# Moving memsets behind the first copies of an attention kernel, and making its first transposes plain matmuls

## The chip, the cores and the metric

One core of a Trainium2 chip. The metric is the device time of one execution in microseconds, median of several executions. The trace of a profiled execution gives the *span*, first to last instruction; it is mostly about 2 us less than the device time of the same run.

## The reference

```python
batch, n_heads, seq_len, head_dim = 4, 8, 1024, 64     # q, k, v; bias is (1, 1, 1024, 1024); all float32
scores = (1 / sqrt(64)) * q @ k.T + bias
attn   = exp(scores - max) / (sum(exp(scores - max)) + 1e-8)
return attn @ v
```

## The kernel before

Heads are worked on in pairs. Scores are computed transposed, in pieces of 512 columns of PSUM, called banks below, three at a time; ScalarE takes the exponential of three banks in one instruction (128x1536, 1.45 us as drawn). The bias enters as a factor, `exp(bias)`, which VectorE multiplies in. v carries a 65th column of ones, so that the last matmul also sums the exponentials. TensorE transposes q and k, and `mask` blanks the other head's half of q.

Everything after the head of the program is emitted by a small model of the engines, written in Python, that picks at each step the instruction that could start first. Its constants `T0` (when the head ends) and `COLD` (until when TensorE costs double) shape that order. This is the head (cut):

```python
nc.sync.dma_start(out=k0f[:, :, :2]...)    # k and q of the first pair, f32, by hardware queues
nc.scalar.dma_start(out=q0f[0]...); nc.sync.dma_start(out=q0f[1]...); nc.sync.dma_start(out=k0f[:, :, 2:]...)
nc.vector.memset(warm[:], 0.0); nc.vector.memset(zeros[:], 0.0)
make_identity(nc, ident[:])
nc.gpsimd.dma_start(kr0 second half); nc.gpsimd.dma_start(qr0 second half); nc.gpsimd.dma_start(btraw first half)
for t in range(2):
    nc.vector.memset(qT0[t * D:(t + 1) * D, 1 - t, :HQ], 0.0)
    for u in range(2):
        nc.vector.memset(mask[t * D:(t + 1) * D, u, :], 1.0 if t == u else 0.0)
nc.gpsimd.memset(vall[:, :, :, D:D1], 1.0)             # the ones, 256 scattered elements per partition
load_v(0); load_qk(1); nc.gpsimd.dma_start(btraw second half); load_v(1); load_qk(2)
wm = ps_s.tile([P, 3, HQ], F32, tag="s", name="wm")
for i in range(6):                                     # warm-up matmuls
    nc.tensor.matmul(wm[:, i % 3, :], zeros[:, :P], zeros[:], start=True, stop=True)
k_first(0, nc.scalar.copy, nc.scalar.copy, "xb")       # cast, transpose, copy of k, chunks 0 and 1
c_a = q_first(0, "xa"); c_b = q_first(1, "xb")         # cast and transpose q of both heads
c_a(); c_b()                                           # copy them out of PSUM
s_fill(0); s_exp(0)                                    # scores and exponential of one bank
k_first(2, nc.vector.tensor_copy, nc.vector.tensor_copy, "xa")
s_fill(1); s_exp(1)                                    # two banks
...                                                    # from here on by the model, three banks each
# the piece of k, chunks 4 to 7, that the fourth exponential needs, is copied in transpose_pe():
nc.vector.tensor_copy(dst[:, half * QC:(half + 1) * QC, :], px[:])          # "the k copy" below
```

The softmax here doesn't subtract the row's maximum and nothing guards it: scores larger than these inputs give would overflow.

## Time and profile before

| | before |
|---|---|
| device time, median of 3 (later 6) runs | 252.03 us (252.06) |
| span of the profiled run | 249.9 us |
| ScalarE busy | 239.0 us, 96% |
| starts of the first four score exponentials | 6.77, 8.43, 9.71, 11.07 us |
| clock of TensorE rises to full | 9.85 us |

From the page of the kernel before: busy time of each engine, and the chain that ended last, by engine.

```profile
PE 228.8 (92%) x3097; PEld 141.1 (56%) x3152; DVE 221.2 (89%) x380; ACT 239.0 (96%) x180; POOL 54.0 (22%) x73
...
ACT 87%; PE 6%; DVE 4%; issue 2%; DVEq 0%; ACTq 0%
```

ScalarE is the engine that the end waits for. From the third exponential (9.71 us) on it runs practically without a break, so the total follows the time at which that unbroken run can begin. What comes before is the head. Its timeline, lines picked; columns: start and duration in us, engine, line, operation, output and inputs, count, and in brackets the idle time before with what ended it.

```profile
3.46 1.70 DVE L258 CAST qr<-q0f 128x256 bf16<-128x256 f32 x2
...
3.54 1.26 POOL L237 MEMSET vall<- 128x256 bf16 x1
...
5.01 0.83 PE L261 MATMUL px<-ident,qr 128*64 128x128 bf16 x8 [0.59 <-DVE qr L258]
...
5.68 0.88 DVE L262 COPY qT<-px 64x512 bf16<-64x512 bf16 x2 [0.53 <-PE px L261]
...
7.36 2.31 PE L129 MATMUL ps<-qT,kT 128*128 128x512 bf16 x5
...
9.61 0.51 PE L89 MATMUL px<-ident,kr 128*64 128x128 bf16 x8
9.71 2.81 ACT L136 ACTIVATE E<-ps 128x1536 bf16<-128x1536 f32 x2 [0.26 <-PE ps L129]
...
10.16 0.42 DVE L102 COPY kT<-px 128x512 bf16<-128x512 bf16 x1 [2.40 <-PE px L89]
```

The two casts of q are of one shape, but the first takes 1.50 us and the second 0.275 (they overlap a little in the 1.70 drawn); the first lies over GpSimd's memset. The five score matmuls from 7.36 us start 0.43 us apart, twice the 0.215 us of those from 11.21 us on: I read that as TensorE at half clock. (Where the trace has a record of a low clock, after its last fall at 248.78 us, the share is 0.5.) The last line is the k copy that the fourth exponential needs: VectorE had been idle for 2.40 us and waited for TensorE's transposes.

### The profile page before, as it was taken

Reading aid. Unit: us, or ns where it says so; the run is one execution under the profiler, and the core shown is the slowest. Engines: PE = TensorE matmul, PEld = TensorE weight load, DVE = VectorE, ACT = ScalarE, POOL = GpSimd, SP = SyncE. Lnnn points to the kernel's source line nnn. Section 1 sums busy time; section 2 is a strip of 40 time slices with the busy share of each in tenths; the row PEclk is TensorE's granted clock in tenths of the full one; section 3 lists DMA queues with packets and bytes.
Section 4 is the critical chain, followed back from the end, with each engine's and each line's share of the span. In section 5 each row is a group of like instructions: output and inputs, shape, how many; then the busy total and the mean of one; then the engine's idle time right before and its main releaser. Section 6 shows DMA issues by size and latency. Waiting matters only on the chain.

```text
span 249.9 us, 7123 instructions
## 1 busy us (share of the span) xinstructions
PE 228.8 (92%) x3097; PEld 141.1 (56%) x3152; DVE 221.2 (89%) x380; ACT 239.0 (96%) x180; POOL 54.0 (22%) x73
## 2 busy tenths in 40 slices
PE   6969999999999999999999999999998999999893
PEld 2346655556566665565565555566665555665552
DVE  7229799899999998999999999999999999998884
ACT  3799999999999999999999999999999999999991
POOL 8753213054004132203150130416000000000000
PEclk9999999999999999999999999999999999999999
DMA  7999979369905987923958194949911102020112
GB/s 153 179 221 183 192 85 149 32 112 154 149 4 104 113 104 114 122 84 52 164 77 93 45 117 95 117 98 108 107 42 43 45 0 88 3 84 3 62 45 64
DMA packets 48175, 23.79 MB, mean 95 GB/s; under 512 B 34448, under 2 KB 44048, under 8 KB 47888
## 3 DMA queue, kind: packets, MB, share of 16 engines
q0 software_dynamic: 42272, 14.42, 52.8%
q1 hardware_dynamic: 5584, 8.72, 9.8%
q8 instruction: 24, 0.39, 0.6%
q10 hardware_dynamic: 288, 0.20, 0.3%
q14 instruction: 7, 0.06, 0.1%
HBM read 29.36 MB, written 8.39 MB: 151 GB/s over the span
## 4 chain that ended last, share of the span: by engine, by line
ACT 87%; PE 6%; DVE 4%; issue 2%; DVEq 0%; ACTq 0%
ACT E L136 84%; PE ps L129 4%; ACT eb L149 3%; PE po L186 1%; DVE mask L236 1%; DVE qr L258 1%; DVE E L155 1%; PE px L89 0%; DVE qT L262 0%; DVE qT L98 0%; PE px L261 0%; DVE E L158 0%; DVE qT L234 0%; DVE oall L206 0%; PE px L254 0%
## 5 line engine op out<-in xcount | busy, mean ns | idle before, releaser
L136 ACT ACTIVATE E<-ps 128x1536 bf16<-128x1536 f32 (+2 forms) x172 | 230.1, 1681 | 3.3 <-PE ps L129 3.3
L129 PE MATMUL ps<-qT,kT 128*128 128x512 bf16 x457 | 135.3, 381 | 11.3 <-ACT E L136 4.6
L186 PEld LDWEIGHTS <-E 128*128 128x128 bf16 x2048 | 82.9, 98 | 39.1 <-DVE E L158 2.7
L158 DVE TENSOR_TENSOR E<-E,eb 128x2048 bf16<-128x2048 bf16 x80 | 96.5, 1217 | 1.0 <-ACT E L136 0.5
L186 PE MATMUL po<-vall,E 128*128 128x65 bf16 x2048 | 92.5, 194 | 2.4 <-DVE E L161 0.8
L129 PEld LDWEIGHTS <-kT 128*128 128x128 bf16 x512 | 45.3, 97 | 43.0 <-issue 8.1
L161 DVE TENSOR_TENSOR E<-E,eb 128x1024 bf16<-128x1024 bf16 x88 | 58.2, 683 | 0.9 <-ACT E L136 0.6
L75 POOL DMA_DIRECT2D kr<-in_k_dram x15 | 10.5, 701 | 94.6 <-PE px L89 92.2
L81 POOL DMA_DIRECT2D vall<-in_v_dram x32 | 28.2, 884 | 6.1 <-DMA btraw<-in_bias_dram 4.0
L206 DVE TENSOR_TENSOR oall<-po,rs 128x256 f32<-128x256 f32 x63 | 26.7, 425 | 2.2
L98 DVE TENSOR_TENSOR qT<-px,mask 128x1024 bf16<-128x1024 bf16 x31 | 21.3, 688 | 4.6 <-PE px L89 4.0
L102 DVE COPY kT<-px 128x512 bf16<-128x512 bf16 x31 | 13.1, 422 | 10.2 <-PE px L89 10.0
L76 POOL DMA_DIRECT2D qr<-in_q_dram x15 | 10.8, 719 | 19.4 <-PE px L89 18.5
L196 DVE RECIPROCAL rs<-po 128x4 f32<-128x4 f32 x64 | 11.3, 177 | 3.4 <-PE po L186 3.1
L89 PEld LDWEIGHTS <-qr 128*64 128x64 bf16 x248 | 7.8, 109 | 9.4 <-issue 8.0
L89 PE MATMUL px<-ident,qr 128*64 128x128 bf16 x248 | 12.8, 225 | 0.1
L89 PE MATMUL px<-ident,kr 128*64 128x128 bf16 x248 | 12.9, 226 | 0.0
L89 PEld LDWEIGHTS <-kr 128*64 128x64 bf16 x248 | 8.0, 110 | 6.1 <-issue 4.2
L149 ACT ACTIVATE eb<-pb 128x2048 bf16<-128x2048 bf16 x4 | 7.5, 1882 | 0.0
L144 PE MATMUL pb<-ident,btraw 128*128 128x128 bf16 x64 | 4.6, 225 | 1.2 <-ACT eb L149 0.6
L144 PEld LDWEIGHTS <-btraw 128*128 128x128 bf16 x64 | 4.5, 146 | 1.6 <-issue 1.3
L155 DVE TENSOR_TENSOR E<-E,eb 128x1024 bf16<-128x1024 bf16 (+1 forms) x6 | 4.6, 775 | 0.6 <-ACT E L136 0.6
(35 smaller groups left out, 22.3 us busy)
## 6 DMA issues: line engine op xcount, KB each, us to landing
out_dram<-oall SPq DMA_DIRECT2D x30, 256.0 KB, 2.0
vall<-in_v_dram POOLq DMA_DIRECT2D x32, 128.0 KB, 5.6
kr<-in_k_dram POOLq DMA_DIRECT2D x15, 256.0 KB, 3.9
qr<-in_q_dram POOLq DMA_DIRECT2D x15, 256.0 KB, 5.3
btraw<-in_bias_dram POOLq DMA_DIRECT2D x2, 1024.0 KB, 10.7
out_dram<-oall SPq DMA_DIRECT2D x3, 128.0 KB, 1.7
k0f<-in_k_dram SPq DMA_DIRECT2D x2, 128.0 KB, 3.3
q0f<-in_q_dram ACTq DMA_DIRECT2D x1, 128.0 KB, 2.5
```

The source lines that it names most:

```text
L81: nc.gpsimd.dma_start(out=vall[:, 2 * pr + t, :, :D], in_=vf[pr, :, t])
L89: nc.tensor.transpose(px[t * D:(t + 1) * D, c, :], src[:, t, half * QC + c, :], ident[:])
L98: nc.vector.tensor_tensor(dst[:, :, half * HQ:(half + 1) * HQ], px.rearrange("p c q -> p (c q)").unsqueeze(1).to_broadcast([P, 2, HQ]), ma ...
L102: nc.vector.tensor_copy(dst[:, half * QC:(half + 1) * QC, :], px[:])
L129: nc.tensor.matmul(ps[:, j, :], kT[:, kc, :], qT[:, h, qh * HQ:(qh + 1) * HQ], start=True, stop=b not in late_bias)
L136: nc.scalar.activation(e_at(slots[g][0], n), open_ps.pop(("S", g))[:, :n, :], ACTF.Exp, scale=scale)
L149: nc.scalar.activation(eb[:, qh, k0:k0 + 4, :], open_ps.pop(("B", qh, k0))[:, :4, :], ACTF.Exp)
L158: nc.vector.tensor_tensor(e, e, eb[:, qh, kc:kc + 2, :].unsqueeze(2).to_broadcast([P, 2, 2, HQ]), op=ALU.mult)
L161: nc.vector.tensor_tensor(e, e, eb[:, qh, kc:kc + 1, :].to_broadcast([P, n, HQ]), op=ALU.mult)
L186: nc.tensor.matmul(acc[:, i, :], e[:, 0, i * P:(i + 1) * P], vall[:, 2 * pr + h, kc, :], start=(kc == 0 and i == 0), stop=(kc == NCH - 1), ...
L196: nc.vector.reciprocal(rs[:], acc[:, :, D:D1])
L206: nc.vector.tensor_tensor(oall[:, c0:c0 + QC, :], acc[:, :, :D], rs[:].to_broadcast([P, QC, D]), op=ALU.mult)
```

## The change

Its intent: keep VectorE and GpSimd free for the first casts by moving the memsets of mask and ones behind the first copies; let the first pair's transposes be plain identity matmuls into f32 PSUM, whose copies are halved over VectorE and ScalarE; and tell the model that TensorE is warm earlier.

```diff
-        for t in range(2):
-            nc.vector.memset(qT0[t * D:(t + 1) * D, 1 - t, :HQ], 0.0)
-            for u in range(2):
-                nc.vector.memset(mask[t * D:(t + 1) * D, u, :], 1.0 if t == u else 0.0)
-        nc.gpsimd.memset(vall[:, :, :, D:D1], 1.0)
-        load_v(0)
+        nc.vector.memset(qT0[D:, 0, :HQ], 0.0)
+        nc.vector.memset(qT0[:D, 1, :HQ], 0.0)
         load_qk(1)
-        (btraw second half, load_v(1), load_qk(2): moved down)
 ...
-            px = ps_x.tile([P, QC, P], BF, tag=tag, name="px")
+            px = ps_x.tile([P, QC, P], F32, tag=tag, name="px")          # the same for k
-                nc.tensor.transpose(px[t * D:(t + 1) * D, c, :], qr0[:, t, c, :], ident[:])
+                nc.tensor.matmul(px[t * D:(t + 1) * D, c, :], qr0[:, t, c, :], ident[:], start=True, stop=True)
-            (one VectorE copy of 512 columns)
+                for c0, eng in ((0, nc.vector.tensor_copy), (m, nc.scalar.copy)):      # m = QC // 2
+                    eng(qT0[...c0 * P:(c0 + m) * P], px[..., c0:c0 + m, :]...)
 ...
         s_fill(1)
         s_exp(1)
+        nc.vector.memset(vall[:, :, :, D:D1], 1.0)
+        for t in range(2):
+            for u in range(2):
+                nc.vector.memset(mask[t * D:(t + 1) * D, u, :], 1.0 if t == u else 0.0)
+        load_v(0); (btraw second half); load_v(1); load_qk(2)
-        COLD = 10500
+        COLD = 6200
-        T0 = 6700.0
+        T0 = 6200.0
```

More of the change, by code (lines that the diff above doesn't have):

```diff
@@ L232 @@
         nc.gpsimd.dma_start(out=btraw[:, :QC, :], in_=bf_[:, :QC, :])
-        for t in range(2):
-            nc.vector.memset(qT0[t * D:(t + 1) * D, 1 - t, :HQ], 0.0)
-            for u in range(2):
-                nc.vector.memset(mask[t * D:(t + 1) * D, u, :], 1.0 if t == u else 0.0)
-        nc.gpsimd.memset(vall[:, :, :, D:D1], 1.0)
-        load_v(0)
+        nc.vector.memset(qT0[D:, 0, :HQ], 0.0)
+        nc.vector.memset(qT0[:D, 1, :HQ], 0.0)
         load_qk(1)
-        nc.gpsimd.dma_start(out=btraw[:, QC:, :], in_=bf_[:, QC:, :])
-        load_v(1)
-        load_qk(2)
         wm = ps_s.tile([P, 3, HQ], F32, tag="s", name="wm")
@@ L250, in k_first @@
             eng_cast(kr0[:, :, cs, :], k0f[:, :, cs, :])
-            px = ps_x.tile([P, 2, P], BF, tag=tag, name="px")
+            px = ps_x.tile([P, 2, P], F32, tag=tag, name="px")
             for c in range(2):
                 for t in range(2):
-                    nc.tensor.transpose(px[t * D:(t + 1) * D, c, :], kr0[:, t, c0 + c, :], ident[:])
+                    nc.tensor.matmul(px[t * D:(t + 1) * D, c, :], kr0[:, t, c0 + c, :], ident[:], start=True, stop=True)
             eng_copy(kT0[:, cs, :], px[:])
@@ L258, in q_first, with copy @@
             nc.vector.tensor_copy(qr0[:, t, :QC, :], q0f[t][:])
-            px = ps_x.tile([P, QC, P], BF, tag=tag, name="px")
+            px = ps_x.tile([P, QC, P], F32, tag=tag, name="px")
             for c in range(QC):
-                nc.tensor.transpose(px[t * D:(t + 1) * D, c, :], qr0[:, t, c, :], ident[:])
-            return lambda: nc.vector.tensor_copy(qT0[t * D:(t + 1) * D, t, :HQ],
-                                                 px[t * D:(t + 1) * D, :, :].rearrange("p c q -> p (c q)"))
+                nc.tensor.matmul(px[t * D:(t + 1) * D, c, :], qr0[:, t, c, :], ident[:], start=True, stop=True)
+            def copy():
+                m = QC // 2
+                for c0, eng in ((0, nc.vector.tensor_copy), (m, nc.scalar.copy)):
+                    eng(qT0[t * D:(t + 1) * D, t, c0 * P:(c0 + m) * P],
+                        px[t * D:(t + 1) * D, c0:c0 + m, :].rearrange("p c q -> p (c q)"))
+            return copy
         k_first(0, nc.scalar.copy, nc.scalar.copy, "xb")
@@ L272 @@
         k_first(2, nc.vector.tensor_copy, nc.vector.tensor_copy, "xa")
-        for g in range(1, 2):
-            s_fill(g)
-            s_exp(g)
-        COLD = 10500
+        s_fill(1)
+        s_exp(1)
+        nc.vector.memset(vall[:, :, :, D:D1], 1.0)
+        for t in range(2):
+            for u in range(2):
+                nc.vector.memset(mask[t * D:(t + 1) * D, u, :], 1.0 if t == u else 0.0)
+        load_v(0)
+        nc.gpsimd.dma_start(out=btraw[:, QC:, :], in_=bf_[:, QC:, :])
+        load_v(1)
+        load_qk(2)
+        COLD = 6200
         EXP, EXP0, QK, AV, TP = 427, 45, 216, 170, 350
```

## The prediction

> **What bounds the kernel now.** ScalarE. The page gives it 239.0 of 249.9 us busy, and the chain of waits runs 87% through it. In the timeline ScalarE goes without a break from the exponential at 9.71 us to 244.9 us; starts farther apart than one instruction takes cost about 1.6 us in all. Then comes a tail of 5 us that the change leaves alone. So the change is worth what it moves the start of that unbroken run, and no more.
>
> **The head, from the timeline.** VectorE runs memsets until 3.42 us. Its first cast of q then takes 1.50 us, the second, same shape, 0.275 us. The first overlaps GpSimd's 1.26 us memset of the ones (3.54 to 4.80), and so I read it as blocked[...]. The chain of waits has this cast as its largest piece (1.51 us) before 6 us. Then: transposes 5.01, copies 5.68 to 6.56 (0.42 us each), first scores 6.15, exponentials 6.77, 8.43, 9.71. The five score matmuls from 7.36 start 0.43 us apart, against 0.21 us after 10 us: the clock is half until about 9.85.
>
> **What changes.**
> 1. Memsets gone from the head. The q casts wait only for their loads: 0.73 + 2.5 = 3.23 us and about 3.84 us (DMA view). I expect 0.3 us each, done by 3.5 and 4.2. The first q transposes move from 5.01 to about 4.2, just behind k's.
> 2. f32 PSUM. VectorE's f32 reads cost about 0.42 us per 256 columns (the output division, same size), as much as 512 bf16 columns now. So halves over two engines only keep the old copy time if they overlap; if the two reads of one bank are ordered, a pair takes about 0.85 us. I take them as ordered: first scores about 5.8 instead of 6.15, first exponential about 6.4 instead of 6.77.
> 3. Plain matmuls. [...] So the clock should rise at 6.43, and five cold score matmuls lose about 0.21 us each. Chance 75%.
> 4. Then exponentials at about 7.2 and 8.2 instead of 8.43 and 9.71. But the moved memsets (four mask pieces, 1.5 us, and the ones, estimated 0.3 us) stand on VectorE before the k copy now at 10.16 us, which the exponential at 11.07 needs. With them done near 9.2, that one starts about 10.1. Net gain about 1.0 us (0.6 if the clock stays cold), all on the critical path.
> 5. Loads reordered, scheduler constants changed: the later order shifts a little. ScalarE has almost no gaps to win there; noise of 0.5 us either way.
>
> **Prediction.** 251.0 us, range 250.1 to 251.9. Faster by over 2%: 0.01; within 2%: 0.98; slower: 0.01.
>
> **What would show it.** First q cast near 0.3 us; score matmuls 0.21 us apart from about 6.5; ordered copies of one bank; VectorE memsets between 7.3 and 9.3 with the next k copy right after; ScalarE unbroken from about 10.
>
> **What would make it wrong.** Clock still cold until 9.85; [...] values or bias landing late, because their loads now stand behind others and perhaps behind VectorE's memset, opening gaps near 14 or 24 us; the new order opening gaps on ScalarE later.

The 6.43 us itself is the rise of before, 9.85 us, less about the 3.41 us that a1 and a3 below show between changes of the clock; that it would rise there is the estimate. The forecast's sum: the third exponential from 9.71 to about 8.2 us by the earlier scores and the clock (five matmuls, 0.21 us each), the fourth from 11.07 to about 10.1 us for the memsets in front of its copy, so about 1.0 us off the 252.03 us of before: 251.0 us.

## The result, and the profile after

| | before | after |
|---|---|---|
| device time, median of 6 runs | 252.06 us (251.59 to 252.77) | 251.89 us (251.66 to 252.32) |
| ratio after to before | | 0.9994 (95%: 0.9975 to 1.0012) |
| span of the profiled run | 249.9 us | 249.9 us |
| first four exponentials | 6.77, 8.43, 9.71, 11.07 us | 6.44, 7.82, 9.10, 11.06 us |
| clock full at | 9.85 us | 10.46 us |

The median of 251.89 us lies just inside the predicted range, which ended at 251.9; that is no success, since the predicted 251.0 us and its gain are not there. Ratios here are the mean time of one kernel's fast runs over that of the other's of the same rounds, so not quite the ratio of the medians. The page's two lines as before:

```profile
PE 232.2 (93%) x3152; PEld 141.9 (57%) x3152; DVE 220.6 (88%) x383; ACT 239.9 (96%) x182; POOL 52.6 (21%) x72
...
ACT 82%; PE 12%; DVE 2%; issue 2%; DMA 1%; DVEq 0%; ACTq 0%
```

The chain has more of TensorE and less of ScalarE than before, but ScalarE is as busy as it was, so this does not size a wait. Six points of the span are about 15 us, and only about 2.7 us of them lie in the first 12.5 us; in the rest the chain was followed through TensorE in more places. The head has to be read from the timeline. The timeline of the head after, the lines that answer to those of before:

```profile
3.31 0.37 DVE L252 CAST qr<-q0f 128x256 bf16<-128x256 f32 x1 [1.40 <-DMA q0f<-in_q_dram]
...
4.28 1.26 PE L255 MATMUL px<-ident,qr 128*64 128x128 bf16 x8
...
4.95 0.42 DVE L260 CAST qT<-px 64x256 bf16<-64x256 f32 x1 [0.57 <-PE px L255]
...
5.40 0.36 ACT L260 CAST qT<-px 64x256 bf16<-64x256 f32 x1 [0.50 <-DVE qT L260]
...
6.75 2.31 PE L129 MATMUL ps<-qT,kT 128*128 128x512 bf16 x5
...
8.16 0.27 DVE L274 MEMSET vall<- 128x256 bf16 x1 [0.88 <-issue]
8.45 1.67 DVE L277 MEMSET mask<- 64x512 bf16 x4
...
9.42 0.64 PE L89 MATMUL px<-ident,qr 128*64 128x128 bf16 x8
...
9.99 1.68 PE L129 MATMUL ps<-qT,kT 128*128 128x512 bf16 x6
10.15 0.42 DVE L102 COPY kT<-px 128x512 bf16<-128x512 bf16 x1
...
11.06 1.45 ACT L136 ACTIVATE E<-ps 128x1536 bf16<-128x1536 f32 x1 [0.51 <-PE ps L129]
```

A wait of ScalarE is counted from the starts in what follows: two exponentials of three banks without a wait between them start 1.33 to 1.36 us apart. The brackets give a little less, because drawn instructions (1.45 us each) overlap.

The first cast is short (0.37 us), and the head is 0.33 us ahead at the first exponential and 0.61 us at the third. All of it is gone at the fourth. Two things stand together there. VectorE comes to the k copy at 10.15 us straight from its memsets, with no idle time, where before it had waited for 2.40 us; the ones have 0.88 us of idleness before them that no wait explains. And TensorE is still at half clock (five score matmuls in 2.31 us again), and now does the q transposes at 9.42 ahead of the score matmuls.

So: **theory V**, VectorE's memsets hold the fourth exponential. **Theory P**, TensorE at half clock, with the new order, holds it. And a **rival R**: such delays are made up later and something else sets the total.

### Reading the clock of runs without a printed trace

The trace records when the clock is raised and lowered; the record begins with the first rise, so before it the slices show full clock and the spacing of matmuls must be read instead. In the profiles the rise and the final fall are mostly 238.93 us apart, as before (9.85 to 248.78) and after (10.46 to 249.39); in a1 and a3 below changes of the clock stand 3.41 us apart (12.74 and 16.15; 4.05, 7.47 and 10.88), and 238.93 us is 70 times 3.413 us. I call a stretch of 3.41 us between such times a *window*; the word stands for these measured distances and says nothing of what decides on the clock. Each run also lists its span and mean granted clock, in which only the half-clock time after the fall is missing (for before, half of 1.09 us in 249.87, which gives 0.998). So *span x (1 - 2 x (1 - clock)) - 238.93* is an estimate of where a window ends in that run, correct to about 0.25 us (the clock has three digits) and only up to whole windows: "8.0" may mean a rise at 4.6, and a run whose clock fell for one window in between looks like one that rose a window earlier or later (a3 below has the place 7.5, and its clock was at half from 7.47 to 10.88). I call it the *place of the window*. For the profiled run of before it gives 249.9 x 0.996 - 238.93 = 9.97; the trace says 9.85.

For 55 runs of the kernel before:

| place of the window | spans of the kernel before |
|---|---|
| 7.1 to 7.7 | 249.8 to 250.1 us (13 runs) |
| 8.0 to 8.6 | 248.9 to 249.0 us (8 runs) |
| 9.1 | 250.5 us (9 runs) |
| 9.4 to 10.6 | 249.8 to 250.5 us (21 runs) |
| not known (clock 1.000) | 250.5 us (4 runs) |

The kernel before has runs 1.0 us shorter than most of its others, and where its clock's windows lie goes with them. Why the 13 runs at 7.1 to 7.7 are not short as well was not traced; a fall as in a3 would give that place. That is as much as the change was to bring, so the traces, and runs at like places, say more here than medians.

### The profile page after: what moved, and what is told of

Its sections match the earlier page's. It is cut to its first block, busy times and chain, and to the rows that moved or that the text cites. A ratio compares the mean times of both kernels' runs of the same rounds, so it can differ in the third digit from the quotient of the medians.

```text
span 249.9 us, 7178 instructions
## 1 busy us (share of the span) xinstructions
PE 232.2 (93%) x3152; PEld 141.9 (57%) x3152; DVE 220.6 (88%) x383; ACT 239.9 (96%) x182; POOL 52.6 (21%) x72
## 4 chain that ended last, share of the span: by engine, by line
ACT 82%; PE 12%; DVE 2%; issue 2%; DMA 1%; DVEq 0%; ACTq 0%
ACT E L136 79%; PE ps L129 8%; ACT eb L149 3%; PE po L186 2%; PE px L89 1%; DMA k0f<-in_k_dram 1%; DVE E L155 1%; DVE E L161 0%; PE px L248 0%; DVE qT L98 0%; DVE oall L206 0%; PE px L255 0%; DVE qT L260 0%; ACT kr L244 0%; DVE rs L196 0%
## 5 line engine op out<-in xcount | busy, mean ns | idle before, releaser
L129 PE MATMUL ps<-qT,kT 128*128 128x512 bf16 x512 | 139.6, 381 | 9.2 <-ACT E L136 4.9
L158 DVE TENSOR_TENSOR E<-E,eb 128x2048 bf16<-128x2048 bf16 x78 | 94.1, 1216 | 9.4 <-ACT eb L149 8.2
L161 DVE TENSOR_TENSOR E<-E,eb 128x1024 bf16<-128x1024 bf16 x92 | 61.0, 682 | 0.9 <-ACT E L136 0.6
## 6 DMA issues: line engine op xcount, KB each, us to landing
btraw<-in_bias_dram POOLq DMA_DIRECT2D x2, 1024.0 KB, 10.6
```

Of the source, the lines that this page charges most:

```text
L129: nc.tensor.matmul(ps[:, j, :], kT[:, kc, :], qT[:, h, qh * HQ:(qh + 1) * HQ], start=True, stop=b not in late_bias)
L158: nc.vector.tensor_tensor(e, e, eb[:, qh, kc:kc + 2, :].unsqueeze(2).to_broadcast([P, 2, 2, HQ]), op=ALU.mult)
L161: nc.vector.tensor_tensor(e, e, eb[:, qh, kc:kc + 1, :].to_broadcast([P, n, HQ]), op=ALU.mult)
```

## The experiments

Times of exponentials, copies and clock are from each run's own trace; "total" is the median of its timed runs, with the ratio to the kernel before. Kernels are compared only within the same rounds. All results were correct.

### a1_masks_twice

```diff
 # the changed kernel
+        (the four mask memsets a second time, behind the first)
```

> The changed kernel with its four mask memsets issued twice: 1.5 to 1.6 us more of VectorE work in front of the k copy that started at 10.15 us. Theory V (those memsets are what the fourth score exponential waits for, and whatever moves it moves the end by as much): that copy at about 11.7, the fourth exponential at about 12.6 instead of 11.06, the whole 1.5 us longer than the changed kernel, about 253.4. Rival R (a delay here is made up later, in gaps of ScalarE): less than 0.5 us longer. Theory P (TensorE alone, at half clock, sets that exponential) would need slack in the copy: under 0.8 us longer.

Measured: k copy at 12.09 us, fourth exponential at 13.09, total 254.24 us (before 252.25; ratio 1.008, 1.006 to 1.010). That is 2.0 us over the kernel before, some more than expected; in this trace the clock rose at 9.33, fell again from 12.74 to 16.15, and rose again. Rival R falls: a delay ahead of the fourth exponential reaches the end in full. That the memsets are what holds it in the changed kernel is not shown by this, since 1.6 us more would outrun any other wait.

### a2_memsets_first, a3_first_old_order, a4_busy

```diff
 # a2: the changed kernel
+        (ones and masks on VectorE in the head, behind the qT0 memsets; none behind s_exp(1))
 # a3: a2 and
-        COLD = 6200; T0 = 6200.0
+        COLD = 10500; T0 = 6700.0
 # a4: a3 and 2, 2 and 4 small matmuls of zeros ahead of k_first, between, and behind the two q_first
+                nc.tensor.matmul(wm[:, i % 3, :P], zeros[:, :P], zeros[:, :P], start=True, stop=True)
```

> The changed kernel with ones and masks on VectorE ahead of the first casts (in its idle 1.9 to 3.3 us); nothing behind the copies. Both theories: first exponentials as in the changed kernel, 6.4, 7.8, 9.1, since the first q cast still ends before TensorE is done with k. Theory V alone: k copy at about 9.7, fourth exponential at about 10.5, total 0.5 us under the changed kernel. Theory P (half clock and the q transposes put ahead of the scores): fourth exponential stays at about 11.0 if the clock is released near 10.4, total the same.

> As the run before, and with the scheduler's two constants of before, so that six score matmuls stand again ahead of the second set of q transposes. Theory V alone: as the run before. Theory P: fourth exponential about 10.8 with a release near 10.4, and earlier the earlier the release; total 0.2 to 0.6 us under the changed kernel.

> As the run before, and with eight small dummy matmuls in TensorE's idle gaps between 3.7 and 5.8 us, so that TensorE is busy nearly without a break from 1.2 us. If the release follows TensorE's business[...]: clock up at some point between 4.6 and 8.0 us[...], third exponential at about 8.4, fourth at about 9.75 instead of 11.06, total about 1.2 us under the changed kernel, 250.7. If the release does not follow it: clock up near 10 again, and as the run before.

| | first, third, fourth exponential | k copy | clock full | total | ratio to before |
|---|---|---|---|---|---|
| a2 | 7.33, 9.93, 11.57 us | 10.50 us | 10.54 us | 252.47 us | 1.0000 (0.9972 to 1.0029) |
| a3 | 6.91, 9.12, 11.07 us | 9.70 us | 4.05 to 7.47, then from 10.88 us | 252.13 us | 0.9988 (0.9960 to 1.0015) |
| a4 | 7.70, 9.94, 11.27 us | 10.12 us | 8.86 us (a share of 0.85) | 251.96 us | 0.9987 (0.9959 to 1.0015) |

All three missed what was expected of them, for one reason: the memset of ones took 1.15 us of VectorE in the head too, 0.88 of it drawn as idleness (from 1.91 to 2.79 us), so the casts waited until 4.79 us. They test the theories badly, but a3 says one thing. Its memsets are out of the way, its k copy is at 9.70, 0.45 us earlier than after the change, and its fourth exponential is still at 11.07: the clock was at half from 7.47 to 10.88. With the memsets gone, theory P has a hold as well; and since a3 has the old order, the half clock alone was enough there. In a4's profiled run the clock was granted at 0.85 for all the rest of it (mean over the run 0.856); that run is not used for more.

### b1_ones_gpsimd, b2_ones_old_order, b3_ones_busy

```diff
 # b1: the changed kernel
-        nc.vector.memset(vall[:, :, :, D:D1], 1.0)
+        nc.gpsimd.memset(vall[:, :, :, D:D1], 1.0)
 # b2: b1 and COLD = 10500, T0 = 6700.0;   b3: b2 and the eight small matmuls of a4
```

> The changed kernel, its memset of ones on GpSimd instead of VectorE, at the same place in the program. What the first batch left: in both places where VectorE does that memset 0.88 us of it stands idle with no wait, so it costs about 1.15 us there and not 0.3. Theory V (VectorE's memsets alone hold the fourth exponential): k copy at about 9.7 instead of 10.15, fourth exponential about 10.6, total 0.4 us under the changed kernel in every run. Theory P (half clock with the q transposes put ahead of the scores holds it as well): no change with a release near 10.4; only runs whose clock is released before about 9 get shorter, by up to 0.6 us.

> As the run before, with the scheduler constants of before, so that six score matmuls again stand ahead of the second set of q transposes. Theory V and theory P both say fourth exponential near 10.6 to 10.8 if the clock is released near 10.4, and down to 9.8 if released before 8; total 0.3 to 0.6 us under the changed kernel, and some spans under 249.0. If the total stays within 0.2 us of the changed kernel, a third cause is missing.

> As the run before, plus the eight dummy matmuls in TensorE's gaps; the first casts are not held up this time, so that they should fit into the gaps and delay nothing (first exponential at 6.4 to 6.5). Clock up between 4.6 and 8.0 us[...]; fourth exponential 9.7 to 10.0; spans near 248.7, total about 1.1 us under the changed kernel. If the dummies only delay the transposes, first exponential at 6.8 or later and no gain over the run before.

| | first, third, fourth exponential | first q cast | k copy | clock full | total | ratio to before |
|---|---|---|---|---|---|---|
| b1 | 6.84, 9.44, 11.19 us | 1.12 us | 10.01 us | 10.27 us | 251.54 us | 0.9981 (0.9948 to 1.0014) |
| b2 | 6.84, 9.44, 10.92 us | 1.36 us | 10.01 us | 9.85 us | 251.48 us | 0.9977 (0.9943 to 1.0010) |
| b3 | 6.54, 8.29, 9.92 us | 1.10 us | 9.01 us | 4.38 us | 251.13 us | 0.9974 (0.9941 to 1.0006) |

No interval excludes 1, so the totals decide nothing. The traces do a little. The q cast is long again as soon as GpSimd does the memset of ones, although that memset is now far behind in the program: it was 1.1 us or longer in all seven traces with that memset on GpSimd, and 0.47 us or shorter in all the others. But an overlap, as in the kernel before, is not what the b traces draw: in b1 the long cast runs from 3.51 to 4.62 us and the memset only from 4.95 us, and b2 and b3 are alike. So that the two go together is shown, and how the one would delay the other is not. The long cast is why the first exponentials of b1 and b2 were late. And b3 has the clock at full from 4.38, its third exponential at 8.29, its fourth at 9.92 and its profiled span at 248.7 us, the last two as expected. Its fourth exponential still waits (0.3 us), for a k copy that starts 0.03 us behind the last mask memset. Taking away part of VectorE's memsets left part of the wait.

### c1_part1, c2_part2

```diff
 # c1: the changed kernel with the first transposes as before (nc.tensor.transpose, bf16 PSUM, one VectorE copy)
 # c2: the kernel before with the plain matmuls, f32 PSUM and halved copies of the change, nothing else
```

> Part 1 of the change alone (memsets and loads moved, new scheduler constants); the first transposes stay transposes into bf16 PSUM with one VectorE copy each. First exponential at about 6.0 instead of 6.44 (no ordered halves); second and third as in the changed kernel or a little earlier, since the second k cast still stands behind both q copies; fourth still held by the ones and masks, at 11.0 (clock release near 10). Total the same as the changed kernel. If the plain matmuls were what pays in the change, it would lose 0.5 us or more against it.

> Part 2 of the change alone, on the kernel before: plain matmuls into f32 PSUM, halved copies; memsets, loads and constants as before. The first q cast again about 1.5 us long. The halves of one bank are ordered, so a pair takes about 0.85 us instead of 0.42: first exponential at about 7.2 instead of 6.77, total 0 to 0.4 us over the kernel before. If plain matmuls raise the clock earlier than transposes do, release at 6.5 in most runs and total 0.3 us or more under the kernel before.

c1: exponentials at 6.12, 7.82, 9.10, 10.96 us, total 252.13 us, ratio 1.0005 (0.9985 to 1.0025). c2: 7.19, 8.51, 9.79, 11.27 us, total 251.84 us, ratio 0.9995 (0.9970 to 1.0021). The exponentials are as expected. Plain matmuls and halves do nothing for the second and third exponential and put off the first by 0.3 to 0.4 us, because the halves run one behind the other (after the change VectorE's from 4.95 to 5.37 us, ScalarE's from 5.40); nor did the clock rise earlier with them (10.47 us in c2 and 10.46 in the changed kernel) than with transposes (10.24 in c1, 9.85 before), though one rise of each says little where the windows move.

### d1_transposes_warm

```diff
 # the kernel before
-        for i in range(6):
-            nc.tensor.matmul(wm[:, i % 3, :], zeros[:, :P], zeros[:], start=True, stop=True)
+        for i in range(64):                                     # wm now bf16
+            nc.tensor.transpose(wm[:, i % 3, :P], ident[:], ident[:])
```

> The kernel before, its six warm-up matmuls replaced by 64 transposes of 128 by 128 without a break (1.3 us to about 8 us at half clock). If transposes do not count as busy for the clock gate[...]: all 64 stay 0.107 us apart[...]. If they do count: clock up between 4.7 and 8.1 us, with transposes 0.055 us apart from there. Either way 2 to 4 us longer than before.

Measured: the clock rose at 4.11 us, when TensorE had done nothing but transposes since 1.36 us. The windows view of the tile they write; the counts in brackets are transposes that run in each microsecond, and one that crosses an edge counts in both.

```profile
1.50:2.50 1.00, 1.00 (x11) 1.00 0.50 146
2.50:3.50 1.00, 1.00 (x12) 1.00 0.89 252
3.50:4.50 1.00, 1.00 (x15) 1.00 0.74 110
4.50:5.50 1.00, 1.00 (x22) 1.00 1.37 200
```

The transposes start 0.107 us apart up to 4.11 us and 0.056 us apart from there on. So in this run the clock rose with nothing but transposes on TensorE. Total 252.21 us against 251.78 before: 0.4 us longer and not the 2 to 4 us expected; with the clock up the 64 transposes were over at 6.4 us.

### e1_late, e3_late_tp_busy

```diff
 # e1: the changed kernel, COLD = 10500, T0 = 6700.0
+        (btraw second half right behind load_qk(1))
+        def late_setup():        # called once, just behind the k copy of chunks 4 to 7
+            (ones and masks on VectorE); load_v(0); load_v(1); load_qk(2)
 # e3: e1 with the transposes and copies of before, and 2 + 2 small matmuls of zeros
```

> The changed kernel with ones and masks still later, behind the k copy that the fourth exponential needs, and the scheduler constants of before; loads of v behind the ones. First three exponentials as in the changed kernel (6.44, 7.82, 9.10 when the loads land as there); k copy at about 9.7 at half clock, at about 8.2 at full clock; fourth exponential at about 10.8 with a release near 10.4, at about 9.7 with one before 8. Total 0.2 to 0.6 us under the changed kernel, more than the ones on GpSimd gained. If loads of v or bias now come late, gaps on ScalarE or VectorE after 18 us show it.

> Everything that the runs so far favour: memsets behind that k copy, transposes and single copies as before, and four dummy matmuls that keep TensorE busy up to the first q transposes. First exponential at about 6.0; clock up before 8 in most runs; third exponential 8.2 to 8.5, fourth 9.6 to 9.9. Span 248.3 to 248.7, total 1.2 to 1.5 us under both kernels. If it is not under the previous run, the clock or the ordered halves were not worth what the traces suggest.

e1: exponentials at 6.53, 7.90, 9.18, 10.67 us, clock full at 9.64, total 251.62 us, ratio 0.9998 (0.9971 to 1.0025). e3: 6.19, 7.55, 8.47, 9.80 us, clock full at 4.76, total 251.67 us, ratio 0.9992 (0.9968 to 1.0017). e3's fourth exponential was 1.27 us ahead of before's, and its profiled span was 250.9 us all the same. Its timeline shows where that went:

```profile
21.54 0.42 PE L188 MATMUL po<-vall,E 128*128 128x65 bf16 x8 [1.60 <-DMA vall<-in_v_dram]
...
22.64 2.79 ACT L138 ACTIVATE E<-ps 128x1536 bf16<-128x1536 f32 x2 [1.12 <-PE ps L131]
```

I had put the first load of v behind the second half of the bias, and TensorE stood waiting for v, with score matmuls behind that wait. This is a flaw of the experiment, and it is also the prediction's warning about loads that stand behind others, come true in a kernel of mine and not in the change. e1 has the same order of loads, but in its trace ScalarE has no later wait, and its fourth exponential follows the third almost without one. Its profiled span was 249.5 us, where the kernel before has 249.8 to 249.9 in nearly all runs at a like place (9.4 to 9.6). Two of its other runs, at 250.4 and 250.9 us with a mean clock of 0.992, took the gain out of the mean; they were not traced.

### f1_after_busy, f2_late_tp, f3_late_tp_busy, f4_before_busy

```diff
 # f1: the changed kernel and 2, 2, 4 and 3 small matmuls of zeros (the last three behind s_fill(0)); memsets where they are
 # f2: late_setup() as in e1, but load_v(0) and the bias stay in place behind load_qk(1), since
+        nc.vector.memset(vall[:, :2, :, D:D1], 1.0)              # in the head: 16 elements
+            nc.vector.memset(vall[:, 2:, :, D:D1], 1.0)          # in late_setup()
 #     transposes and copies of before; COLD = 10500, T0 = 6700.0
 # f3: f2 and 2, 2 and 3 small matmuls;   f4: the kernel before and 2, 7, 4 and 3 small matmuls
```

> The changed kernel with eleven small dummy matmuls in TensorE's gaps up to the second k transposes, so that the clock is up before 8 us in nearly every run. Theory V (VectorE's ones and masks, 0.88 us idle with them, hold the k copy): third exponential at 8.2 to 8.5 but k copy still at 9.7 to 10.1 and fourth exponential at 10.4 to 10.8, total at most 0.5 us under the changed kernel. Theory P (half clock alone): fourth exponential at 9.6 to 9.9, total 1.2 us under.

> Transposes and single copies as before, masks and most ones behind the k copy, ones of the first pair in the head so that the first v load stands ahead of the second bias load; scheduler constants of before; no dummies. First exponential 6.0 to 6.2; with a release near 10, fourth at 10.6 to 10.8 (TensorE at half clock holds it), span 249.5; in runs with an early release 9.7 and span 248.4. Median 0.2 to 0.6 us under the changed kernel. No gap on ScalarE near 20 us, unlike the run with v behind the bias.

> As f2, with seven dummy matmuls. Both causes gone: clock up before 8 us, third exponential 8.2 to 8.5, fourth 9.6 to 9.9, spans 248.3 to 248.8 in nearly all runs, total 1.2 us under both kernels. If it stays within 0.4 us, something after the fourth exponential takes the gain back.

> The kernel before with sixteen small dummy matmuls in TensorE's gaps, nothing else: the clock up before 8 us. First exponential still at 6.8[...], third at about 8.9 instead of 9.71, fourth at about 10.2 instead of 11.07, total 0.7 to 0.9 us under the kernel before: an early clock pays there, since no memsets stand ahead of that k copy. If the total stays, the clock is not what the head of the kernel before waits for.

| | first, third, fourth exponential | k copy | clock full | total | ratio to before |
|---|---|---|---|---|---|
| f1 | 6.30, 8.06, 10.81 us | 9.90 us | 4.50 us | 252.75 us | 1.0024 (1.0002 to 1.0046) |
| f2 | 5.78, 8.06, 9.39 us | 8.14 us | 4.37 us | 250.38 us | 0.9939 (0.9914 to 0.9964) |
| f3 | 6.11, 8.67, 10.00 us | 8.75 us | 5.44 us | 250.70 us | 0.9953 (0.9930 to 0.9977) |
| f4 | 6.48, 8.81, 10.14 us | 8.89 us | 4.89 us | 251.02 us | 0.9968 (0.9940 to 0.9996) |

f1 and f2 have the third exponential at the same 8.06 us and the clock at full from nearly the same time. f2's fourth follows as soon as ScalarE is free, and its k copy waits for TensorE:

```profile
7.14 3.71 ACT L138 ACTIVATE E<-ps 128x1024 bf16<-128x1024 f32 x3 [0.76 <-PE ps L131]
...
8.14 0.42 DVE L102 COPY kT<-px 128x512 bf16<-128x512 bf16 x1 [1.24 <-PE px L89]
```

f1's comes 1.42 us later than f2's. The chain of waits of f1, its columns start, us, and what ran:

```profile
6.60 0.42 DVE kT L253
7.03 0.89 issue
7.92 0.27 DVE vall L282
8.19 0.01 issue
8.20 0.48 DVE mask L285
...
9.38 0.48 DVE mask L285
9.87 0.03 issue
9.90 0.43 DVE kT L102
10.33 0.05 issue
10.38 0.40 PE ps L129
10.78 0.02 issue
10.81 2.79 ACT E L136 x2
```

The chain goes through every one of the memsets and the idleness before the ones. Theory V holds as soon as the clock is up: with the memsets where the change put them an early clock brings nothing. f4 is the counterpart: the kernel before, with an early clock and no memsets ahead of its k copy, was 0.3% shorter, the interval just clear of 1. f2 gained more than expected (1.5 us under before), and part of that may be luck: five of its six runs have an early place of the window. f3, with dummy matmuls on top, gained no more than f2. f1 as a whole was longer than before, more than its trace explains; three of its six runs have a mean clock of 0.987 to 0.990, as if it had fallen once more for a window, as in a1. That was not traced and stays open.

### g1_late_only, g2_late_tp_again

```diff
 # g1: the changed kernel and late_setup() as in f2: plain matmuls, halves and scheduler constants of the change stay
 # g2: the file of f2 once more
```

> The changed kernel with its memsets behind that k copy (and the 16 ones that the first pair needs in the head, so that the first v load keeps its place), all else as the change has it. If the memsets are what took the gain: fourth exponential 9.5 to 10.0 and spans 248.4 to 249.0 in runs whose clock is up before 9 us; at 10.6 to 11.0 and spans 249.5 to 250.0 in the others, where TensorE at half clock is next in line; median 0.3 us or more under the changed kernel. If not: spans 249.5 to 250.2 whatever the clock, as the changed kernel.

> The same file as the fastest version so far, once more. If its gain was its own: median span at least 0.6 us under the kernel before of the same rounds again, and every run of it at or under the kernel before in runs with the clock released at the same time. If it was luck with the windows: median within 0.4 us of before.

g1: exponentials at 6.93, 8.30, 9.30, 10.64 us, clock full at 8.84, total 251.40 us, ratio 0.9986 (0.9948 to 1.0025), so the total alone is unclear. Its loads landed late (first q cast at 3.92 us), and its fourth exponential was later than the 9.5 to 10.0 expected for a rise before 9 us, but the wait is gone, as its timeline shows:

```profile
8.30 5.13 ACT L138 ACTIVATE E<-ps 128x1024 bf16<-128x1024 f32 x4 [0.77 <-PE ps L131]
...
9.65 0.42 DVE L102 COPY kT<-px 128x512 bf16<-128x512 bf16 x1 [1.88 <-PE px L89]
...
10.89 0.26 DVE L281 MEMSET vall<- 128x240 bf16 x1 [0.82 <-issue]
```

ScalarE runs on from the second exponential without a stop, and VectorE again waits 1.88 us for TensorE at the k copy. g2: exponentials at 6.08, 7.77, 9.05, 10.78 us, clock full at 10.37, total 250.71 us, ratio 0.9949 (0.9908 to 0.9989): f2's gain came again, this time with a profiled run of the late clock, whose fourth exponential waited 0.40 us for TensorE.

Spans by the place of the window put the four versions side by side (runs with a place that can't be told left out):

| place | before | changed | g1 | f2 and g2 |
|---|---|---|---|---|
| 7.3 to 8.9 | 248.9 to 250.1 us | 249.6 us | 248.3, 248.8 us | 248.1 to 248.4, once 248.8 us |
| 9.0 to 9.6 | 249.8 to 250.5 us | 250.0, 250.2 us | 248.9, 249.4, 249.7 us | - |
| 9.9 to 10.6 | 249.9 to 250.0 us | 249.9, 250.0 us | 250.0 us | 249.4 to 249.8 us |

At the late place all of them meet at 249.4 to 250.0: there TensorE at half clock can hold the fourth exponential whatever the memsets do, as in the traces of g2 and a3. At the early place g1 and f2 go down to 248.1 to 248.8; the changed kernel's one run there stands at 249.6. One run is thin, and its place may hide a fall of the clock as in a3; the evidence that the memsets hold it at an early clock is f1's trace.

## Why the prediction was wrong

1. **ScalarE bounds the kernel, and only the head counts.** Right. a1 shows a delay before the fourth exponential reaching the end in full.
2. **The first q cast is long because of GpSimd's memset; without it 0.3 us.** Right in the number: 0.37 us, and the cast was long in exactly the traces with that memset on GpSimd. The runs show that the two go together (1.1 us or longer against 0.47 or shorter), not why, and in b1 to b3 the memset is drawn only after the long cast has ended (in b1 from 4.95 us, the cast to 4.62).
3. **First transposes at 4.2, a pair of halves 0.85 us, scores at 5.8, first exponential at 6.4.** Right: 4.28, 0.82 us (4.95 to 5.76), 5.82, 6.44. That the two reads of one bank would be ordered was the assumption; in the trace ScalarE's half waits for VectorE's (0.50 us of idle time, ended by it).
4. **"So the clock should rise at 6.43."** Wrong. It rose at 10.46. The step took the windows of one trace for fixed in time. The traces show that they are not: one and the same file had its first rise at 4.37 us in f2 and at 10.37 in g2, 6.00 us apart and so not a whole number of windows of 3.41 us, and others rose at 4.05, 5.44, 8.86, 9.64 and 10.54. In d1 the clock rose at 4.11 us with nothing but transposes.
5. **"With them done near 9.2, that one starts about 10.1. Net gain about 1.0 us (0.6 if the clock stays cold)."** Wrong, and this is the step that lost the prediction: even with a cold clock it still promised 0.6 us. The term for VectorE's memsets was mis-sized. The ones were put at 0.3 us and cost 1.15 (0.88 us drawn idle, 0.27 busy) for 256 scattered elements per partition, where 512 neighbouring ones of a mask took 0.485 us; 240 scattered ones took 1.08 us in f2 and g1 (0.82 idle, 0.26 busy), which makes it about 4.5 ns each, an estimate from these two. With the masks the memsets lasted from 7.28 to 10.12 us, so the k copy began at 10.15, where it had begun before (10.16). f1 shows that this alone holds the fourth exponential at 10.81 when all else is early; g1, that the wait goes when the memsets go behind that copy.
6. **"The later order shifts a little ... noise."** Not quite. The new constants put eight q transposes, 0.43 us of them at half clock (9.42 to 9.85 us), ahead of the scores that the fourth exponential needs. In a late-clock run TensorE would have come to the third of those score matmuls only at about 10.6 us even without the memsets (it started at 10.64). That time is an estimate from its starts in the trace (9.99 and 10.39 us for the two before it, with the rise at 10.46). So in the profiled run both causes stood at the same time, and taking away one would not have been enough there; a3, with the memsets gone but the clock half, still had its fourth exponential at 11.07. Nor would the 0.6 us for a cold clock have come in full: with the memsets behind the k copy and a late rise, the fourth exponential stood at 10.67 (e1) and 10.78 us (g2), 0.3 to 0.4 us ahead of before.

Where the gain went, then: off the first three exponentials it was real (0.61 us), and a new wait at the fourth took all of it, VectorE's memsets in the traces that have them there (after the change, c1 and f1) and TensorE's half clock as well in a run with a late rise. The plain matmuls and halved copies gained nothing measurable (c1, c2). What stays open: what decides when the clock rises; why f1 lost more than its trace shows; what the new order costs by itself, since no run is the changed kernel with the old constants alone; why the first q cast is long (1.1 us or more) with the memset of ones on GpSimd, even where the two aren't drawn to overlap; and how much of the residual 0.5% of f2 is due to each of its parts.

## What to carry to other kernels

Work moved off one wait lands in front of another: before moving an instruction, ask which waiting instruction of the same engine then stands behind it, and put it behind that one instead; f2 does, and is the fastest version here. Size a moved instruction by what it keeps its engine from, not by its drawn length (the ones: 0.27 us drawn, 1.15 us taken), and look for idleness without a wait ahead of it. And when a clock whose rise is not tied to the program's start (4.37 and 10.37 us for one file) moves the runs by as much as the change, compare traces and runs at like places of the clock before medians.
